# Layer A's probabilities, two heads of four turned by DMA as half-precision pairs

## The chip, the cores and the metric

The kernel runs on one core of one Trainium2 chip. The metric is the device time of one execution in microseconds; the time of a kernel is the median of its runs. A profile shows one execution, with the busy time of each engine: PE (TensorE, matmuls and the transposes made by matmul), PEld (its weight loads, which overlap), DVE (VectorE), ACT (ScalarE), POOL (GpSimd) and SP (SyncE, whose queue issues all of this kernel's DMAs).

## The reference

Two attention layers over 2048 prompt tokens and 64 sample tokens of width 1024. Each layer does `x + W_out(attn(RMSNorm(x)) * silu(gate))`, with q, k, v and gate from one input projection and RMS-normed q and k. Layer A (the one that changes) has 16 query heads on 2 key/value heads of width 64; a query of chunk c (64 tokens) sees its own chunk and the two before it, with a bucketed relative-position bias and a sink per head. Layer B has 16 heads with their own keys and values and sees 9 chunks.

```
def attend(q, k, v, bias, valid, sinks):
    s = jnp.einsum('bqkgd,bskd->bkgqs', qg, k).astype(jnp.float32) * (dh ** -0.5)
    s = s + bias.reshape(kv, g, tq, tk)
    s = jnp.where(valid, s, NEG_INF)
    sink = sinks.astype(jnp.float32).reshape(kv, g, 1, 1)
    m = jnp.maximum(jnp.max(s, axis=-1, keepdims=True), sink)
    p = jnp.exp(s - m)
    p = p / (jnp.sum(p, axis=-1, keepdims=True) + jnp.exp(sink - m))
    o = jnp.einsum('bkgqs,bskd->bqkgd', p.astype(v.dtype), v)
```

All arrays are float32. The kernel keeps that precision by holding a value as a high part (the value rounded to a matmul type) and a low part (what the rounding left), and by multiplying the parts.

## The kernel before

**Work items.** Layer A runs over four quarters of the heads (`qd`, four query heads each, two quarters to a key/value head) and, in each, over nine units: eight of 256 prompt tokens and one of the 64 sample tokens (`u == NU`). A prompt unit has two items of 128 tokens. That makes 64 prompt items and 4 sample items. All prompt items but the first tile of each quarter attend to two key tiles of 128 (their own and the one before); the four first tiles attend to one.

**The filler.** The projections run ahead of the attention and fill the gaps in it. `Filler` holds a generator of projection matmuls, and `filler.to(mark)` issues them on PE until the mark. PE's order is written out by hand (`manual_schedule` for PE); the instructions of the other engines and of the SP queue are put in order by the scheduler, from the order of the program and its simulated times, and then run in that order on their engine.

**One iteration of layer A's `pipeline`**, for item i: `scores(items[i])`; projections up to 0.3 of the iteration; `values(items[i-1])`; projections; in the first quarter `keys(items[i+2])`; projections up to 0.8; `turned(items[i+2], items[i-1])`; projections up to 0.95; `outputs(items[i-1])`; projections to the end.

- `scores`: 8 matmuls into two PSUM banks (tag `sa`), then for heads 0 and 1 and again for heads 2 and 3 the minimum with the bias and the sink on DVE (line 1213), and the exponential on ACT (line 1219), which writes p in float32 and adds up each row. Each pair of heads has one `p` tile; there are three `p` buffers.
- `values`: for each key tile 4 transposes on PE (line 904, 128x128 in float32) into one `sa` bank, then the high part by ACT (`ph`, line 871) and the low part by DVE (`pl`, line 872), for all four heads at once.
- `outputs`: for each key tile two matmuls of 512 columns (lines 1255 and 1256), with the values as the stationary operand. The values are held in one tile with high and low halves, both float32r (`VT`), so that rows 0 to 63 of the result hold the high half's product and rows 64 to 127 the low half's. `finish_pairs` adds the two, multiplies by the gate (line 1316 on POOL) and stores the result.
- `turned`: transposes of q and of the gate, their evacuation, and two small DMAs of q (line 1171) for item i+2.

The first projection, `first`, runs at the start, and `take_kv` splits the values by ACT and POOL (`split_v`, lines 847 and 848).

**Layer B** already holds its probabilities, in seven of its eight head pairs, in the other form: ACT writes the high part in float16 (line 1554), POOL the low part (line 1555), and one DMA with transposition (line 1563, tile `pt`) turns both; line 1660 multiplies them with values in float16. There the products come three steps after the DMA is asked for.

Of the kernel before, what the change touches and what calls it, by code (L numbers as in the profile page):

```python
# [9 lines left out]
F32 = mybir.dt.float32  # L10
# [43 lines left out]
TURNED = (0, 1)  # L54

@with_exitstack
def hybrid_encoder_kernel(
# [104 lines left out]
    row = const([P, 64], "scrow")[0:1]  # L162
    scanned, pending = [], []
# [697 lines left out]

    KA = const([P, SEQ], "KA", F16)
    KB = const([P, SEQ], "KB", F16)
    VT = t("values", [P, NT, 2, P], 1, F32R)
# [14 lines left out]

    def split_at(x, c):  # L880
        return x[:, :c], x[:, c:]
# [43 lines left out]
    held["chain"] = []  # L925
# [48 lines left out]
    def layer_a():  # L974
# [4 lines left out]
        def add_unit(qd, place, unit):  # L979
# [30 lines left out]
            def take_kv(it, ps):  # L1010
# [4 lines left out]
                split_v(n, v, VS[:, 1] if last else VT[:, tt])  # L1015
# [23 lines left out]
            def first():  # L1039
# [85 lines left out]
        def turned(it, done):  # L1125
# [13 lines left out]
            if done is not None:  # L1139
                done.gt = gate_t(tp[:, 256 : 256 + 2 * m].rearrange("p (j s) -> p j s", j=2), m)  # L1140
# [32 lines left out]
        def scores(it):  # L1173
# [33 lines left out]
            for j in range(2):  # L1207
# [4 lines left out]
                for h in (2 * j, 2 * j + 1):  # L1212
# [4 lines left out]
                    )  # L1217
                for h in (2 * j, 2 * j + 1):
# [4 lines left out]
            bg.anchor(mi, ex)  # L1223
            nc.vector.reciprocal(sm[:n], sm[:n])
# [7 lines left out]

        def values(it):
            qd = it.qd
# [13 lines left out]
        def outputs(it):  # L1248
# [5 lines left out]
            for c, (vt, kn) in enumerate(it.vts):  # L1254
                nc.tensor.matmul(O[:, : 4 * n], vt, hi[c], start=c == 0, stop=False)
                nc.tensor.matmul(O[:, : 4 * n], vt, lo[c], start=False, stop=c == m - 1)  # L1256
# [9 lines left out]
        def pipeline():  # L1266
            N = len(items)
            for i in range(-3, N + 1):
# [10 lines left out]
                filler.to(c0 + 0.3 * (end - c0))  # L1279
                if 0 <= i - 1:  # L1280
# [747 lines left out]
```

## Time and profile before

| | |
|---|---|
| Time, median of 3 runs | 2119.95 us (2118.64 to 2123.06) |
| The profiled execution | 2123.14 us, span 2121.3 us |
| Layer A's first quarter, with the start | 0 to 200 us of the span |
| Layer A's other three quarters | 200 to 645 us |
| Layer A's output projection | 645 to 870 us |
| Layer B's attention | 870 to 1970 us, then its output projection |
| Busy over the span | PE 96%, DVE 71%, ACT 68%, POOL 54% |
| Mean granted TensorE clock | 0.991 |

In a group of instructions the columns are line, engine, operation, output and inputs, shapes and count, then the busy time in microseconds and the mean of one in nanoseconds, then the idle time before them. In a timeline they are the start and the length in microseconds. A matmul's bar is longer than the time for which it holds the array, since matmuls are pipelined; the distance between starts tells what one costs.

### The profile page before, as it was taken

To read this page: it belongs to the slowest core of one execution; us is meant where nothing else is said; L and a number is where in the kernel's file an instruction comes from. 1 tells how busy PE (TensorE), PEld (TensorE's weight loads), DVE (VectorE), ACT (ScalarE), POOL (GpSimd) and SP (SyncE) were. 2 spreads that over 40 slices of the span, in tenths; PEclk is the share of its full clock that TensorE was granted. 3 is DMA by queue.
4 is the path that set the end of the run, shared out by engine and by line. 5 is a ranking of instruction groups with operands and counts; after the bars stand their busy time and mean duration, and the time that the engine had idled before them with its cause. 6 is when DMAs were issued, how large, how long until landed. Compare 5 with 4: busy or idle time off the path is not lost.

```text
span 2121.3 us, 40864 instructions
## 1 busy us (share of the span) xinstructions
PE 2046.8 (96%) x12951; PEld 1470.7 (69%) x12951; DVE 1498.7 (71%) x4049; ACT 1440.8 (68%) x3640; POOL 1143.7 (54%) x1621
## 2 busy tenths in 40 slices
PE   8999999999999999998999999999999999999999
PEld 6788788878888999655655555555555555557788
DVE  7778778768667554687768777787877778678542
ACT  6878878767777332466677677786867777677330
POOL 5655544433445445775367576676766767575000
PEclk9999999999999999999999999999999999999999
DMA  8856545766544666744469789897897969678763
GB/s 276 274 172 213 173 157 189 215 174 212 165 149 132 212 205 200 247 148 155 138 166 225 175 191 232 169 239 180 199 216 169 254 159 212 152 152 197 215 200 115
DMA packets 509593, 404.21 MB, mean 191 GB/s; under 512 B 302064, under 2 KB 446848, under 8 KB 509344
## 3 DMA queue, kind: packets, MB, share of 16 engines
q1 hardware_dynamic: 509376, 401.60, 70.1%
q8 instruction: 102, 1.67, 0.3%
q14 instruction: 115, 0.94, 0.1%
HBM read 257.59 MB, written 73.43 MB: 156 GB/s over the span
## 4 chain that ended last, share of the span: by engine, by line
PE 59%; DVE 12%; ACT 10%; DMA 6%; issue 6%; POOL 5%; SPq 0%; ACTq 0%; POOLq 0%; DVEq 0%
PE pj L713 10%; PE pj L715 10%; PE pj L714 10%; PE pj L1871 5%; PE pj L1873 5%; PE pj L1872 5%; PE o L1660 2%; PE sa L904 2%; PE tp L904 2%; DVE p L1502 2%; ACT values L1554 2%; PE sb L1498 2%; ACT p L1514 1%; PE sb L1499 1%; PE o L1256 1%
## 5 line engine op out<-in xcount | busy, mean ns | idle before, releaser
L713 PE MATMUL pj<-wh,xx 128*128 128x512 f16 (+2 forms) x1648 | 641.9, 389 | 6.0 <-ACT pb L736 2.3
L715 PE MATMUL pj<-wh,xx 128*128 128x512 f16 (+2 forms) x1648 | 624.3, 379 | 1.3 <-POOL xx L598 1.3
L714 PE MATMUL pj<-wh,xx 128*128 128x512 f16 x1024 | 389.4, 380 | 0.8 <-DVE wh L503 0.8
L1555 POOL TENSOR_TENSOR values<-p,values 128x640 f16<-128x640 f32 (+2 forms) x224 | 281.5, 1259 | 177.5 <-ACT values L1554 172.9
L1514 ACT ACTIVATE p<-p,nm 128x640 f32<-128x640 f32 (+5 forms) x264 | 199.3, 755 | 199.5 <-DVE nm L1507 150.3
L1871 PE MATMUL pj<-xx,wh 128*128 128x264 f32 (+1 forms) x1024 | 291.4, 285 | 8.4 <-DVE res L1877 3.9
L1872 PE MATMUL pj<-xx,wh 128*128 128x264 f32 (+1 forms) x1024 | 288.9, 282 | 0.0
L1502 DVE CUSTOM_DVE_ANT_0 p<-sb,BT 128x640 f32<-128x640 f32 (+5 forms) x272 | 196.6, 723 | 94.8 <-PE sb L1499 91.1
L714 PE MATMUL pj<-wl,xx 128*128 128x512 f32 (+1 forms) x624 | 234.6, 376 | 3.0 <-DVE wl L503 3.0
L598 POOL TENSOR_TENSOR xx<-xraw,xx 128x528 fp32r<-128x528 f32 (+4 forms) x144 | 185.4, 1305 | 90.8 <-ACT xx L597 84.1
L813 POOL TENSOR_TENSOR f<-f,mhalf 128x4 f32<-128x4 f32 (+2 forms) x187 | 190.4, 1019 | 11.8
L715 PEld LDWEIGHTS <-xx 128*128 128x128 f16 x1024 | 100.5, 98 | 124.5 <-issue 2.8
L1316 POOL TENSOR_TENSOR o<-gt,o 128x256 f32<-128x256 f32 (+1 forms) x132 | 103.6, 784 | 152.2 <-ACT p L1219 92.5
L818 DVE TENSOR_TENSOR pa<-pa,f 128x256 f32<-128x256 f32 (+3 forms) x221 | 145.6, 661 | 54.4 <-POOL f L813 49.9
L795 POOL TENSOR_TENSOR sq<-pa 128x256 f32<-128x256 f32 (+2 forms) x187 | 115.0, 615 | 115.1 <-ACT pa L749 80.1
L1219 ACT ACTIVATE p<-p,nm 128x257 f32<-128x257 f32 (+2 forms) x272 | 134.4, 497 | 47.4 <-DVE nm L1213 40.0
L714 PEld LDWEIGHTS <-xx 128*128 128x128 f16 x1024 | 100.5, 98 | 82.5 <-issue 4.7
L713 PEld LDWEIGHTS <-xx 128*128 128x128 f16 x1024 | 100.6, 98 | 80.7 <-ACT xx L597 1.5
L1554 ACT CAST values<-p 128x640 f16<-128x640 f32 (+2 forms) x224 | 147.3, 658 | 5.0
L1873 PE MATMUL pj<-xx,wl 128*128 128x264 f32 x512 | 145.8, 285 | 0.5 <-DVE wl L496 0.5
L1873 PE MATMUL pj<-xx,wh 128*128 128x264 f16 x512 | 142.7, 279 | 1.0 <-DVE wh L493 1.0
L1213 DVE CUSTOM_DVE_ANT_0 p<-sa,BT,nsink 128x256 f32<-128x256 f32 (+2 forms) x272 | 117.5, 468 | 35.7 <-PE sa L904 29.8
(282 smaller groups left out, 5028.9 us busy)
## 6 DMA issues: line engine op xcount, KB each, us to landing
xx<-xsb SPq DMA_DIRECT2D x112, 512.0 KB, 4.3
xx<-xsa SPq DMA_DIRECT2D x88, 512.0 KB, 4.7
xraw<-oga SPq DMA_DIRECT2D x64, 264.0 KB, 3.8
xraw<-ogb SPq DMA_DIRECT2D x64, 264.0 KB, 3.9
xsa<-xx SPq DMA_DIRECT2D x32, 512.0 KB, 4.3
wl<-in_w_in_b_dram SPq DMA_DIRECT2D x64, 256.0 KB, 5.0
wraw<-in_w_in_b_dram SPq DMA_DIRECT2D x56, 256.0 KB, 3.6
xraw<-in_x_dram SPq DMA_DIRECT2D x40, 256.0 KB, 4.2
```

Of the source, the lines that this page charges most:

```text
L598: nc.gpsimd.tensor_tensor(lo, rv, wide(hi), op=ALU.subtract)
L713: nc.tensor.matmul(ps[:n, :C], xh, wh, start=k == 0, stop=False)
L714: nc.tensor.matmul(ps[:n, :C], xh, wl, start=False, stop=False)
L715: nc.tensor.matmul(ps[:n, :C], xl, wh, start=False, stop=k == KC - 1)
L813: nc.gpsimd.tensor_tensor(fv, fv, mhalf[:n, :H], op=ALU.pow)
L1502: mi = nc.vector.tensor_tensor_reduce(out=p[r, :nk], in0=S[r, o : o + nk], in1=b, op0=ALU.add, op1=ALU.min, scale=1.0, scalar=3e38, accum_ ...
L1514: ex = nc.scalar.activation(p[:n, :nk], p[:n, :nk], AF.Exp, scale=-1.0, bias=it.nm[:n, c : c + 1], accum_out=it.sm[:n, c : c + 1],)
L1554: hi = nc.scalar.copy(two[:, :, 0, :], pv)
L1555: lo = nc.gpsimd.tensor_tensor(two[:, :, 1, :], pv, two[:, :, 0, :], op=ALU.subtract)
L1871: nc.tensor.matmul(ps[:, :OT], wh, oh, start=k == 0, stop=False)
L1872: nc.tensor.matmul(ps[:, :OT], wh, ol, start=False, stop=False)
L1873: nc.tensor.matmul(ps[:, :OT], wl, oh, start=False, stop=k == KC - 1)
```

## The change

For prompt items the probabilities of heads 0 and 1 (`TURNED_A = (0,)`, the first pair) no longer go through PE. After the exponential ACT copies them to float16 into a ring of three places, POOL writes the low part beside them, and one DMA with transposition on SP (`turn_a`) turns both parts of both heads: 4 m blocks of 128x128 for m key tiles. It is issued in the item's own iteration, ahead of `values` of the item before. Heads 2 and 3 are still transposed on PE, into one bank for both key tiles, and split by ACT and DVE, now into float16. `outputs_a` has matmuls of 256 columns in float16: first those of heads 2 and 3, high and low part and key tile by key tile, then those of heads 0 and 1 that read the turned tile.

The exponent gets log(2^14) added on DVE (one small instruction for each pair of heads), so that p is scaled; the row sums take up the same factor. The values are held as float16 high and low parts with one scale for the tensor, a power of two from the largest entries of the value weights (`value_top`, `value_across`, `value_scales`, all in the first unit and at the start of the second); the gate takes it out again. Since that scale is not known in the first unit, the value splits of its two tiles are put off to the second. They are now made by ACT and DVE. The tile `values` has the same bytes as before; its second half is the ring. Sample items are as before.

```diff
+    def value_top(ws):
+        for c, (w, _) in enumerate(ws[::2]):
+            nc.vector.tensor_reduce(
+                most[:, 80 + c : 81 + c], w.h[:, :, P:].bitcast(F32), axis=AX.XY, op=ALU.max,
+                apply_absolute_value=True,
+            )
+        nc.vector.tensor_reduce(
+            top[:, 10:11], most[:, 80:84], axis=AX.X, op=ALU.max, apply_absolute_value=True
+        )
+
+    def value_across():
+        ps = tp_bank()
+        nc.tensor.transpose(ps[0:1, 0:P], top[:, 10:11], ident)
+        m, e, r, o = row[:, 40:41], row[:, 41:42], row[:, 42:43], row[:, 44:46]
+        nc.vector.tensor_reduce(m, ps[0:1, 0:P], axis=AX.X, op=ALU.max)
+        nc.vector.tensor_scalar(m, m, 1e-12, 1.0, op0=ALU.max, op1=ALU.mult)
+        powers(m, e, r)
+        times(o[:, 0:1], r, VB)
+        times(o[:, 1:2], e, 0.5 / VB)
+
+    def value_scales():
+        ps = tp_bank()
+        nc.tensor.matmul(
+            ps[:, 0:2], ones[0:1, 0:1].to_broadcast([1, P]), row[:, 44:46], start=True, stop=True
+        )
+        nc.vector.tensor_copy(sva, ps[:, 0:2])
...
-    VT = t("values", [P, NT, 2, P], 1, F32R)
+    V16, ring = split_at(t("values", [P, 4 * NT * P], 1, F16), 2 * NT * P)
+    VT = V16.rearrange("p (a b c) -> p a b c", b=2, c=P)
+    held["ring"] = 0
...
-                split_v(n, v, VS[:, 1] if last else VT[:, tt])
+                if last:
+                    split_v(n, v, VS[:, 1])
+                else:
+                    held["v"].append((VT[:, tt], v.rearrange("p (h d) -> p h d", d=HD)))
+                if u == 1 and it is mine[0]:
+                    value_scales()
+                while u and held["v"]:
+                    vt, vv = held["v"].pop(0)
+                    split_to(vt[:, :, 0:HD], vt[:, :, HD:P], vv, sva[:, 0:1])
...
+                    if i == 5:
+                        value_top(st.wkv)
                     if i == 7:
                         token_scales(unit, xc, tp_bank())
...
                 for it, o in zip(mine, qgs):
                     take_qg(it, o[0])
+                value_across()
...
+                if u != NU:
+                    mi = nc.vector.tensor_scalar(
+                        nm[:, 2 * j : 2 * j + 2], nm[:, 2 * j : 2 * j + 2], math.log(PB), 1.0,
+                        op0=ALU.add, op1=ALU.mult,
+                    )
...
+            if u != NU:
+                held["ring"] = r = (held["ring"] + 1) % 3
+                m = nk // P
+                it.two = two = ring[:, 1024 * r :][:, : 512 * m].rearrange(
+                    "p (c l h k) -> p l c h k", c=m, l=2, h=2
+                )
+                for y, j in enumerate(TURNED_A):
+                    hi, lo = (two[:, l, :, 2 * y : 2 * y + 2] for l in range(2))
+                    pv = it.pe[j][:, :, :nk].rearrange("p h (c k) -> p c h k", k=P)
+                    nc.scalar.copy(hi, pv)
+                    nc.gpsimd.tensor_tensor(lo, pv, hi, op=ALU.subtract)
+                it.two = ring[:, 1024 * r :][:, : 512 * m]
...
+        def turn_a(it):
+            if it.unit[0] == NU:
+                return
+            it.pt = t("pt", [P, 2 * HALF], 2, F16)[:, : it.two.shape[1]]
+            nc.sync.dma_start_transpose(it.pt.rearrange("p (c q) -> p c q", q=P), it.two)
+
+        def values_a(it):
+            m = len(it.vts)
+            ph, pl = (t(x, [P, 5, 256], 2, F16) for x in ("ph", "pl"))
+            it.hi, it.lo = [], []
+            heads = [h for h in range(4) if h // 2 not in TURNED_A]
+            if heads:
+                PT = psum_a("sa", 512, 4)
+                PTv = PT.rearrange("p (c h k) -> p c h k", c=2, h=2)
+                for c in range(m):
+                    for x, h in enumerate(heads):
+                        transpose(PTv[:, c, x], it.pe[h // 2][:, h % 2, c * P : (c + 1) * P])
+                a, b = (x.rearrange("p a b -> p (a b)")[:, : m * 256] for x in (ph, pl))
+                bg.anchor(*split_to(a, b, PT[:, : m * 256]))
+                it.hi, it.lo = ([x[:, 256 * c : 256 * c + 256] for c in range(m)] for x in (a, b))
+
+        def outputs_a(it, O):
+            m = len(it.vts)
+            w = 256
+            heads = [h for h in range(4) if h // 2 not in TURNED_A]
+            todo = []
+            for c, (vt, kn) in enumerate(it.vts):
+                for l in range(2):
+                    if heads:
+                        todo.append((O[:, heads[0] * P : heads[0] * P + 256], vt, (it.hi, it.lo)[l][c]))
+                    todo.append(
+                        (O[:, 2 * P * TURNED_A[0] :][:, :w], vt, it.pt[:, (2 * c + l) * w : (2 * c + l + 1) * w])
+                    )
+            todo.sort(key=lambda x: x[2].tensor is it.pt.tensor)
+            for y, x in enumerate(todo):
+                nc.tensor.matmul(*x, start=y == 0, stop=y == len(todo) - 1)
...
                 filler.to(c0 + 0.3 * (end - c0))
+                if 0 <= i < N:
+                    turn_a(items[i])
                 if 0 <= i - 1:
                     values(items[i - 1])
```

More of the change, by code (lines that the diff above doesn't have):

```diff
@@ L54 @@
 TURNED = (0, 1)
+TURNED_A = (0,)
 @with_exitstack
@@ L162, in hybrid_encoder_kernel @@
     row = const([P, 64], "scrow")[0:1]
+    sva = const([P, 2], "sva")
     scanned, pending = [], []
@@ L922, in low_queries @@
         return Q2[turn[0] % 2]
-    held["chain"] = []
+    held["chain"], held["v"] = [], []
     class Filler:
@@ L1139, in turned @@
             if done is not None:
-                done.gt = gate_t(tp[:, 256 : 256 + 2 * m].rearrange("p (j s) -> p j s", j=2), m)
+                done.gt = gate_t(
+                    tp[:, 256 : 256 + 2 * m].rearrange("p (j s) -> p j s", j=2), m,
+                    0.5 if done.unit[0] == NU else sva[:, 1:2],
+                )
             if it is not None:
@@ L1253, in outputs @@
             m = len(it.vts)
-            for c, (vt, kn) in enumerate(it.vts):
-                nc.tensor.matmul(O[:, : 4 * n], vt, hi[c], start=c == 0, stop=False)
-                nc.tensor.matmul(O[:, : 4 * n], vt, lo[c], start=False, stop=c == m - 1)
+            if it.unit[0] != NU:
+                outputs_a(it, O)
+            else:
+                for c, (vt, kn) in enumerate(it.vts):
+                    nc.tensor.matmul(O[:, : 4 * n], vt, hi[c], start=c == 0, stop=False)
+                    nc.tensor.matmul(O[:, : 4 * n], vt, lo[c], start=False, stop=c == m - 1)
             finish_pairs(
```

7 lines of the change are left out of this document (5 added, 2 removed).

## The prediction

> **What bounds the kernel now.** I read the page's engine totals first, then layer A's two stretches, then PE's starts in time.
>
> ```profile
> PE 2046.8 (96%) x12951; PEld 1470.7 (69%) x12951; DVE 1498.7 (71%) x4049; ACT 1440.8 (68%) x3640; POOL 1143.7 (54%) x1621
> core 0: us, PE busy (x) PEld busy (x) DVE busy (x) ACT busy (x) POOL busy (x), PEclk, DMA share, GB/s
> 0.00:200.00 200.00, 185.45 (x1101) 155.91 (x1102) 147.36 (x522) 157.34 (x423) 113.76 (x172) 0.98 0.73 232
> 200.00:645.00 445.00, 439.98 (x2412) 356.26 (x2411) 325.59 (x958) 341.03 (x952) 200.00 (x383) 0.99 0.59 179
> ```
>
> From 200 to 645 us, layer A's last three quarters, PE has 5 us idle in 445, while ACT is busy 77% (341.03/445), DVE 73%, POOL 45% and DMA 59%. Busy bars overlap, so the starts have to say whether the array itself is full. One item, from its scores to the next item's scores:
>
> ```profile
> 401.68 0.39 PE L1255 MATMUL o<-ph,values 128*128 128x512 f32 x1
> 401.91 0.39 PE L1256 MATMUL o<-pl,values 128*128 128x512 f32 x1
> 402.14 0.28 PE L1202 MATMUL sa<-KB,q 128*128 128x256 f16 x1
> 402.26 0.27 PE L1203 MATMUL sa<-KB,q 128*128 128x256 f16 x1
> 402.37 0.27 PE L1202 MATMUL sa<-KB,q 128*128 128x256 f16 x1
> ...
> 405.10 1.03 PE L904 MATMUL sa<-ident,p 128*128 128x128 f32 x8
> 405.89 0.48 PE L713 MATMUL pj<-wh,xx 128*128 128x512 f32 x1
> 406.20 0.39 PE L714 MATMUL pj<-wl,xx 128*128 128x512 f32 x1
> ...
> 409.87 0.39 PE L1255 MATMUL o<-ph,values 128*128 128x512 f32 x1
> ...
> 410.81 0.28 PE L1202 MATMUL sa<-KB,q 128*128 128x256 f16 x1
> ```
>
> A float32r matmul of 512 columns costs 0.23 us (401.68 to 401.91), a float16 one of 256 columns 0.11 (402.26 to 402.37). Eight transposes with the projection matmul behind them take 1.10 (405.10 to 406.20), so 0.87 without its 0.23: 0.109 each. The item lasts 8.67 (402.14 to 410.81), and its work adds up to that: 24 projections at 0.23 (5.52), 8 scores (0.88), 8 transposes (0.87), 4 of q and gate (0.44), 4 products (0.92): 8.63. PE is full; its time is the stage's time.
>
> **What the change takes from PE.** A full prompt item loses 4 of 8 transposes, 4 x 0.109 = 0.44. Its 4 products at 0.23 (0.92) become 8 at 0.11 (0.88): 0.04 less. Together 0.47. There are 15 full items in each quarter, 60 x 0.47 = 28.2; the four with one key tile give half, 1.0. The sum is **29 us** off PE.
>
> The Trainium skill (TensorE: Matmul & The Clock Gate, Part 4: PE-mode transpose) gives about 275 ns for one such transpose inside a kernel; by that price the 248 removed would be 68 us. The row of this trace has that length as the bar's, and the starts decide:
>
> ```profile
> L904 PE MATMUL sa<-ident,p 128*128 128x128 f32 x496 | 64.5, 272 | 0.0
> ```
>
> **What it moves to the other engines.** Layer B does the same steps, so most have a row.
>
> ```profile
> L871 ACT CAST ph<-sa 128x512 fp32r<-128x512 f32 x124 | 68.0, 588 | 19.7 <-PE sa L904 19.0
> L872 DVE TENSOR_TENSOR pl<-sa,ph 128x512 fp32r<-128x512 f32 x124 | 81.0, 681 | 0.7 <-ACT ph L871 0.4
> L1554 ACT CAST values<-p 128x640 f16<-128x640 f32 x168 | 121.7, 724 | 3.7
> L1555 POOL TENSOR_TENSOR values<-p,values 128x640 f16<-128x640 f32 x168 | 237.2, 1415 | 127.5 <-ACT values L1554 123.4 <-issue 1.3 <-DMA pt<-values 1.1
> L1507 DVE TENSOR_SCALAR nm<-nm 128x1 f32<-128x1 f32 x224 | 32.0, 143 | 1.1
> ```
>
> Per full item ACT swaps one of two high parts (588 ns) for the copy of p: 512 columns, some 0.58 by 724 x 512/640. Nothing. DVE loses one low part (681) and gains two additions (2 x 143): 0.39 less. POOL gains 1415 x 512/640 = 1.13. Over an item of 8.67 - 0.47 = 8.20, POOL goes from 3.90 (45% of 8.67) to 5.03, 61%; ACT stays at 6.68, 81%; DVE falls to 72%. All are covered by PE's 8.20. The value splits shift about 0.3 us each, 16 times, from POOL to DVE, once in the kernel.
>
> DMA needs a sum. Two stretches of 300 us, layer A's first (300 to 600) and layer B's second (1100 to 1400), and the start (30 to 130):
>
> ```profile
> q1 hardware_dynamic: 38468, 55.49, 61.2%
> q1 hardware_dynamic: 109331, 58.71, 86.4%
> pt<-values SPq DMA_TRANSPOSE x74, 4.0
> q1 hardware_dynamic: 19122, 26.64, 82.2%
> ```
>
> Layer A's plain traffic takes 183.6 us (61.2%) for 55.49 MB, 3.3 us per MB. In layer B 74 turns of at most 0.33 MB (128 x 640 x 2 parts x 2 bytes) are some 24 MB; the other 34.5 cost 114 us, which leaves 145 of 259 for the turns, about 2.0 each. Layer A's is 0.26 MB: 1.55 us of all engines, per item 18% more. After 200 us DMA goes from 59% to about 80%, under the 86% with which layer B runs. In the start it goes from 82% to 96% (an item there has 24 projections of 512 columns and 24 of 256, some 11 us: 14%). That is the one place where I charge for it: 100 us hold 9 items, 14 us of transfers into 18 us of slack. I take **3 us**, from 0 (all fits) to 10 (most of it stalls PE).
>
> The Trainium skill (DMA: Bandwidth & Descriptors, Latency and other measured facts) gives 261 GB/s for a transposing DMA on non-contiguous data; by that the turn would take 1.0 us and the start would reach only 91%, and I would charge nothing there. The trace's 0.33 MB in 2.0 us is dearer, and I keep it.
>
> **When the turned tile lands.** `outputs` now waits on a DMA, in PE's order, and everything on PE stands behind it. ACT and POOL at the same item, layer B's turn, and its landing:
>
> ```profile
> 407.60 0.20 ACT L1219 ACTIVATION_READ_ACCUMULATOR p<-p,nm 128x1 f32 x1
> 408.22 0.61 POOL L1226 TENSOR_TENSOR G<-pb,sm 128x256 f32<-128x256 f32 x1 [1.65 <-DVE sm L1224]
> 408.79 0.61 POOL L795 TENSOR_TENSOR sq<-pa 128x256 f32<-128x256 f32 x1
> 410.37 1.01 POOL L813 TENSOR_TENSOR f<-f,mhalf 128x4 f32<-128x4 f32 x1
> L1563 SPq DMA_TRANSPOSE pt<-values x224: 1167/1363/5339, 1059.6 to 1964.1; - x112
> DMA to landing us min/median/max: 2.3/3.7/9.2
> ```
>
> The exponentials of the item scored at 402.14 end at 407.8. The copy ends at 408.4 (0.58), the low part at 409.5 (1.13), or near 411 if POOL has G and the square first. SP then spends 1.36 on the issue, and landing takes 3.7 in the median: 413 to 416. The item's products stand one item after 409.87, at 418.5. So the chain is 11 to 14 us long and may be 16.4, which is 1.89 periods; at the new 8.20 it may be 15.5. Usually covered by 2 to 4 us; the 9.2 us landing overshoots. Behind the turn on SP wait the loads of `xx`, q and bias rows and the stores of `oga`, by about 1.4 us of issue and what POOL is late; they are asked for a unit or an item ahead. POOL's G, squares and powers wait 1.1 longer behind the low part; what they feed, `turned`, comes most of an item later. For such small lateness I take **2 us**, from 0 to 8. Below nothing is possible too: a turned `p` tile comes free without waiting for line 904 in the next item, and the second pair's softmax can start earlier; since PE is full that earns no time.
>
> **The start.** Four reductions of 256 columns, a small one, a transpose, six tiny DVE steps, a matmul and a copy come in before the second unit's values. The nearest rows:
>
> ```profile
> L809 DVE TENSOR_REDUCE f<-sq 128x4 f32<-128x256 f32 x176 | 72.3, 414 | 24.1 <-POOL sq L795 23.8
> 12.28 0.15 DVE L143 TENSOR_SCALAR qsc<-qkg 128x2 f32<-128x2 f32 x1
> 28.75 0.50 PE L714 MATMUL pj<-wl,xx 128*128 128x512 f32 x1 [2.97 <-DVE wl L503]
> ```
>
> 4 x 0.41 + 8 x 0.15 = 2.8 us of DVE, where PE already waits 2.97 for DVE. I take **3 us**; 0 if the reductions fall into DVE's gaps, 6 if PE's transpose and matmul wait for the tiny steps as well.
>
> **The sum.** 29 - 3 - 2 - 3 = 21 us less. The profiled execution, 2123.14 with a span of 2121.3, lies 3.2 above the median of 2119.95; 2123.14 - 21 = 2102 on its own footing, and on the median's, which I predict, **2099 us**. With every charge at nothing it is 2091; with all at their ends (10, 8, 6) 2115.
>
> **The rivals.**
>
> ```profile
> SPq L1563 <- POOL G L1539: 71.0, 24, 5.0
> who waited for it (us, times):
>   ACT o L1311: 12.1, 10
>   POOL values L1555: 1.1, 1
> ```
>
> *The turn decides (slower).* Place: the wait for `pt` ahead of `outputs_a`'s last four matmuls. Each period is then the chain divided by 1.89. From 15.5 us of mean chain on PE waits, and from 16.4 on (8.67 an item) the change loses. With landings near 7 us instead of 3.7, an SP queue that holds the turn back 1 us, and POOL's late case, 14 becomes 18.3; then the period would be 9.68, and 62 items x (9.68 - 8.67) = +63, with the start's 3 some 2186. A milder case, chain 17 and period 9.0, gives 62 x 0.33 + 3 = +23: 2143, the price I put on it. For it: SP's order is fixed ahead, and in layer B SP stands waiting for POOL in front of line 1563. Against it: among those that wait for layer B's `pt`, the last rows above, there is no PE, at a higher DMA load, though with three steps between. 15%.
>
> *PE is not the bound (no change).* ACT, DVE and their handoffs set the item, and what PE saves turns into waits: 29 - 29, with the start's 3 and the DMA's -2 at most, 2120 to 2125; I put 2121. PEld is busy only 356 of 445 us, 80%. Against it: starts 0.23 apart in a row and 8.63 of 8.67 accounted for. The Trainium skill (Trainium Kernel Development and Optimization, Best Practices) has the rule behind it: judge by weight loads, not by matmul busy time. By that, a fifth of the stage would be open. The starts don't bear it out. 7%.
>
> *The half-precision products cost more (smaller gain).* Eight matmuls load weights eight times. If each cost 0.17 instead of 0.11, the 0.47 would vanish; line 1202's starts, each with its own weights, speak against it. 3%, near 2121 too.
>
> **Chances.** Forecast 75%, of which all is faster. Turn decides 15%, slower. No gain 10%: half within 0.2% (4 us, about what a measurement of this kernel can tell from no change), a third slower, the rest faster. So faster 0.77, same 0.05, slower 0.18. The range runs from 2089 (all charges nothing, less 2 for the spread of runs) to 2125, which takes in the no-gain cases and leaves out the turn's.
>
> **What the changed profile would show.** Line 904's `sa` transposes by 248 fewer; the item from scores to scores near 8.2 us; line 1660's kind of row, 256 columns, 0.11 apart; no PE wait on `pt` above 2 us in all; POOL near 60% and DMA near 80% after 200 us; PE's starts lagging by about 3 us after the first 40. Wrong would be a PE idle row released by `pt` or by `xx`, or an item still at 8.6.

## The result, and the profile after

The changed kernel takes 2129.19 us (median of 5 runs, 2128.62 to 2134.18), the kernel before 2118.64 (5 runs beside them, 2115.68 to 2123.06). The ratio is 1.0055, 95% interval 1.0037 to 1.0073: slower, where 2099 us was forecast, with a range of 2089 to 2125. The profiled execution of after is one of 2129.19 us, with a span of 2127.4 and a granted clock of 0.992.

The page's engine totals of after:

```profile
PE 2021.7 (95%) x12954; PEld 1442.1 (68%) x12954; DVE 1506.4 (71%) x4145; ACT 1440.7 (68%) x3644; POOL 1215.0 (57%) x1669
```

The two stretches of layer A, with the columns shown before (us, then busy time and instructions of PE, PEld, DVE, ACT and POOL, then granted clock, DMA share, GB/s):

```profile
0.00:200.00 200.00, 176.31 (x1085) 146.88 (x1086) 153.72 (x561) 157.57 (x421) 124.97 (x169) 0.99 0.85 247
200.00:645.00 445.00, 421.17 (x2411) 334.73 (x2410) 322.61 (x1002) 336.65 (x947) 250.35 (x426) 1.00 0.76 205
```

PE is busy for 25 us less in the whole span (29 were worked out). But from 200 to 645 us, with nearly the same number of matmuls (2411 and 2412), it is busy for 421 us where it was for 440, in the same 445. The saving turned into waits. What PE waited for in that stretch (us in total, times, longest):

```profile
PE o L1330 <- DMA pt<-values: 7.5, 6, 1.6
PE tp L935 <- DVE pa L847: 6.5, 6, 3.3
PE o L1330 <- DVE pl L906: 5.3, 13, 0.7
```

In the names, `pa` is the q of a coming item, which DVE multiplies by its norm before PE transposes it for `turned`, and `pb` is its gate. None of these three rows stood in that table of before but `pa`, once, with 2.4 us. One item of the last quarter, scores to scores, shows the commonest of them (timeline of after: start, length):

```profile
592.75 0.27 PE L1247 MATMUL sa<-KB,q 128*128 128x256 f16 x1
...
596.24 0.48 DVE L1258 CUSTOM_DVE_ANT_0 p<-sa,BT,nsink 128x256 f32<-128x256 f32 x1
...
596.65 0.69 DVE L1264 TENSOR_SCALAR nm<-nm 128x2 f32<-128x2 f32 x2
...
597.37 0.51 ACT L1269 ACTIVATE p<-p,nm 128x257 f32<-128x257 f32 x1 [0.86 <-DVE nm L1264]
...
598.86 0.50 ACT L1269 ACTIVATE p<-p,nm 128x257 f32<-128x257 f32 x1
...
599.36 0.56 ACT L905 CAST ph<-sa 128x512 f16<-128x512 f32 x1
...
599.95 0.69 DVE L906 TENSOR_TENSOR pl<-sa,ph 128x512 f16<-128x512 f32 x1
...
600.70 0.27 PE L1330 MATMUL o<-pl,values 128*128 128x256 f16 x1 [0.31 <-DVE pl L906]
...
601.46 0.27 PE L1247 MATMUL sa<-KB,q 128*128 128x256 f16 x1
```

Both additions stand on DVE behind all four minima (596.65). The exps of the first pair wait for them and then run four in a row to 599.3. The cast of the other pair's high part comes behind the exps, the low part behind the cast, and the products of the item before wait for the low part. Then come the next scores, 8.71 after the last ones. There is no wait on the turned tile in this quarter. In before, each of the first pair's exps started right behind its own minimum, and the casts of the high parts came between the two pairs (the item of the prediction, scored at 402.14):

```profile
404.01 0.08 DVE L1213 DVE_READ_ACCUMULATOR2_ANT nm<- 128x1 f32 x1
...
404.19 0.51 ACT L1219 ACTIVATE p<-p,nm 128x257 f32<-128x257 f32 x1 [0.86 <-DVE nm L1213]
...
405.73 1.07 ACT L871 CAST ph<-sa 128x512 fp32r<-128x512 f32 x2 [0.45 <-PE sa L904]
...
405.95 0.48 DVE L1213 CUSTOM_DVE_ANT_0 p<-sa,BT,nsink 128x256 f32<-128x256 f32 x1 [0.23 <-PE sa L904]
...
406.69 0.52 ACT L1219 ACTIVATE p<-p,nm 128x257 f32<-128x257 f32 x1
```

By line and shape, the additions, the exps of the full items, the transposes left on PE and the new work on ACT and POOL:

```profile
L1264 DVE TENSOR_SCALAR nm<-nm 128x2 f32<-128x2 f32 x128 | 39.1, 327 | 0.6
...
L1269 ACT ACTIVATE p<-p,nm 128x257 f32<-128x257 f32 x240 | 119.9, 502 | 59.2 <-DVE nm L1264 57.1 <-POOL p L1256 1.7 <-POOL f L842 0.4
...
L935 PE MATMUL sa<-ident,p 128*128 128x128 f32 x248 | 37.4, 272 | 0.0
L1283 ACT CAST values<-p 128x512 f16<-128x512 f32 x60 | 36.7, 612 | 0.1
...
L1284 POOL TENSOR_TENSOR values<-p,values 128x512 f16<-128x512 f32 x60 | 70.7, 1179 | 5.6 <-ACT values L1283 4.2 <-DMA row<-vec 0.7
```

An addition took 327 ns in the mean, not the 143 that it was priced at, and ACT stood 57.1 us in front of the exps until an addition was done (in before 38.2 us, until a minimum was). The casts and the low parts lie near the forecast 580 and 1130 ns, and the transposes are the 248 fewer. The queue's shares of DMA time, from 300 to 600 us and from 30 to 130:

```profile
q1 hardware_dynamic: 71018, 64.83, 79.7%
q1 hardware_dynamic: 24317, 27.43, 92.6%
```

### The profile page after: what moved, and what is told of

Same layout as the page of the kernel before. It is cut to its first block, busy times and chain, and to the rows that moved or that the text cites. A ratio compares the mean times of both kernels' runs of the same rounds, so it can differ in the third digit from the quotient of the medians.

```text
span 2127.4 us, 41090 instructions
## 1 busy us (share of the span) xinstructions
PE 2021.7 (95%) x12954; PEld 1442.1 (68%) x12954; DVE 1506.4 (71%) x4145; ACT 1440.7 (68%) x3644; POOL 1215.0 (57%) x1669
## 4 chain that ended last, share of the span: by engine, by line
PE 46%; DVE 17%; ACT 12%; DMA 9%; issue 8%; POOL 6%; SPq 1%; ACTq 0%; POOLq 0%; DVEq 0%
PE pj L742 7%; PE pj L744 7%; PE pj L743 7%; PE pj L1977 4%; PE pj L1979 4%; PE pj L1978 4%; PE o L1766 3%; ACT p L1269 2%; DVE p L1258 2%; PE sb L1604 2%; PE sb L1605 2%; DVE pa L847 2%; DVE p L1608 2%; DVE o L1421 1%; PE tp L935 1%
## 5 line engine op out<-in xcount | busy, mean ns | idle before, releaser
L847 DVE TENSOR_TENSOR pa<-pa,f 128x256 f32<-128x256 f32 (+3 forms) x221 | 150.0, 680 | 56.6 <-POOL f L842 50.3
L824 POOL TENSOR_TENSOR sq<-pa 128x256 f32<-128x256 f32 (+2 forms) x187 | 116.6, 624 | 98.9 <-ACT pa L778 79.7
L742 PEld LDWEIGHTS pj<-wh,xx 128*128 128x128 f32 x624 | 117.7, 189 | 25.0 <-ACT pb L765 7.5
```

The lines of the kernel that those rows point to most:

```text
L742: nc.tensor.matmul(ps[:n, :C], xh, wh, start=k == 0, stop=False)
L847: nc.vector.tensor_tensor(sv, sv, fv.unsqueeze(2).to_broadcast([n, H, HD]), op=ALU.mult)
```

## The experiments

Two theories stood at the beginning. **Theory A**: the loop scores, minima, additions, exps, cast, low part, products, next scores became longer than PE's work, because the exps wait for the additions. **Theory B**: the turn by DMA is what is late, by its own length and by SP's order. Ratios are to the kernel before on the same chip.

**Without the two additions** (noadd):

```diff
-                if u != NU:
-                    mi = nc.vector.tensor_scalar(
-                        nm[:, 2 * j : 2 * j + 2], nm[:, 2 * j : 2 * j + 2], math.log(PB), 1.0,
-                        op0=ALU.add, op1=ALU.mult,
```

> Leaves out the two additions of log(2^14) per prompt item, so layer A's p is not scaled. Theory A (a loop of handoffs sets the item: scores, minima and additions on DVE, all four exponentials on ACT, then the cast ph, then pl on DVE, then the products and the next scores): the first pair's exponentials start 2 us earlier, and items of the last quarter fall from 8.70 to 8.2-8.4 us; about 15 us less than the changed kernel, near 2113. Theory B (the turn: SP's queue, the DMA load and the wait for pt set it): no change, near 2129.

2118.73 us, 0.9981 (0.9971 to 0.9991), and the last quarter's items last 8.2 us instead of 8.7. Two instructions of a third of a microsecond are worth 0.74%, some 16 us. In the profiled executions of after and noadd these lie in the second quarter (8.7), the last (2.8) and the stretch between layer A's last item and layer B's first turn (5.3); so the loop of the steady items is shown for a part of them.

**The second pair's softmax asked for after `values`** (split):

```diff
-            for j in range(2):
+            def pair(j):
...
+            pair(0)
...
+            def second():
+                pair(1)
...
                     values(items[i - 1])
+                if 0 <= i < N:
+                    second()
```

> The second pair's softmax is asked for after the split of the item before (values), and the turned pair's copy and low part follow the first pair's exponentials at once; the order on PE is the same. Theory A: the cast ph stands between the two pairs' exponentials on ACT, as before the change; the wait for pl goes, items of the last quarter at 8.2-8.3 us, near 2110. Theory B: only the turn is earlier; the waits for pt in the third quarter (some 9 us) go, the last quarter stays at 8.70, near 2123.

A miss: 2133.85 us, 1.0051 (1.0036 to 1.0067), items still 8.7. In its trace DVE's order still has both additions together behind the fourth minimum. ACT's order did follow: the cast of the high part now stands between the two pairs of exps. But the first pair's exps still wait for the additions, and so the cast starts 6.6 us after the item's scores, as in after, and the products still wait for the low part. The order in the program fixed the order on one engine and not on the other, and the run left the wait as it was.

**Layer B's bias rows moved out of the third quarter** (spread), into layer A's output projection:

```diff
-                        if qd == 2 and 1 <= place <= 4:
-                            spread(1, place - 1)
...
+                    if layer == 0 and half == 0 and m == 1 and j < 7:
+                        spread(1, j, 2)
```

> Layer B's bias rows are spread (32 DMAs of 191.5 KB) during layer A's output projection instead of its third quarter, so that SP and the DMA engines are freer beside the turns. Theory A: the pt waits of the third quarter go, but its items then meet the same loop at 8.7: 5 us less, near 2124. Theory B: 10 us or more less, 2119 or below.

2137.11 us, 1.0068 (1.0055 to 1.0082). The third quarter's mean item (its length over its 17 items, the sample item among them) went from 8.93 to 8.63 us, so the rows do stand in its way, but the output projection lost more than that.

**Without the turn by DMA** (noturn; the products read the parts unturned):

```diff
-            it.pt = t("pt", [P, 2 * HALF], 2, F16)[:, : it.two.shape[1]]
-            nc.sync.dma_start_transpose(it.pt.rearrange("p (c q) -> p c q", q=P), it.two)
+            it.pt = it.two
```

> Leaves out the DMA with transposition: the products read the unturned parts from the ring, so these two heads' products are of other data; everything else is there. Theory A: no wait for pt, but items of the last quarter still take 8.70: near 2124. Theory B: what the change takes from PE comes through: near 2100.

2131.15 us, 1.0032 (1.0019 to 1.0045); the last quarter stays at 8.7. The turn explains a small part only, as theory A has it.

**The first pair's addition ordered ahead of the second pair's minima** (addorder):

```diff
+                    if u != NU and h == 2:
+                        behind(mi.ins, add.ins)
```

> All computation of the changed kernel is kept; on VectorE the second pair's two minima are ordered behind the first pair's addition, which stands behind both minima of its pair, so that the first pair's exps can start while the second pair's minima are still being made. Theory A (the loop scores, four minima, both additions, four exps, cast, low parts, products, next scores sets the item): the exps of the first pair start about 1 us earlier (two minima of 0.4 us and an addition of 0.33), the cast of the second pair's high parts with them, the last quarter's period falls from 8.70 to about 8.2 to 8.3, the waits of the exps on nm from 57 to under 25 us, and the time to about 2113 to 2117. Rival (it is the additions' own time on VectorE, 39 us in all, not their place): the period stays near 8.7 and the time near 2129.

The last quarter's steady items fell to 8.2 to 8.3 us, as theory A said, and yet the time was 2132.88, 1.0062 (1.004 to 1.0085). In its trace the earlier quarters are longer: PE waits 7.4 us for `pa` and 7.2 for the turned tile from 200 to 645 us, and the first quarter's items last 11.69 us in the mean where they last 11.23 in after. What follows is narrower than hoped: the loop in the steady items is mended, and the earlier quarters lose more than the last one gains. The edit makes DVE's order stiffer everywhere; whether that is the reason isn't shown.

**The kernel before with the two additions alone** (before_add):

```diff
+                if u != NU:
+                    mi = nc.vector.tensor_scalar(
+                        nm[:, 2 * j : 2 * j + 2], nm[:, 2 * j : 2 * j + 2], math.log(PB), 1.0,
+                        op0=ALU.add, op1=ALU.mult,
```

> The kernel before with nothing changed but the two additions to nm, one per pair, ahead of the exps; the probabilities are then larger by a constant factor that the division by their sum takes out. Theory A: there the loop has a slack of its own (the exps of the first pair start right behind two minima, and PE is full), so that the additions take a part of it and the rest is lost: the period of the last quarter rises by 0 to 0.6 us, the time to between 2119 and 2140, and if the additions stand behind all four minima here too, to about 2135. Rival (the additions cost only together with the cast and the low parts of the second pair): no change, 2119.

2131.84 us, 1.0067 (1.0046 to 1.0087). The additions cost some 14 us in the old kernel as well. Here, though, the steady items stayed at 8.7. In the profiled execution, 6 us longer than that of before, the loss lies in the first quarter (11.87 us an item for 11.38), with PE waiting for `pl`, `pb` and `pa`.

**A constant value scale** (const), with no work for it at the start:

```diff
+    nc.vector.memset(sva[:, 0:1], 64.0)
+    nc.vector.memset(sva[:, 1:2], 0.5 / 64.0)
...
-                    value_scales()
...
-                        value_top(st.wkv)
...
-                value_across()
```

> The changed kernel with the value scale a constant, 64, and its two reciprocal factors constants too: no largest value is taken, none is handed across the partitions, and the values are split as they arrive. What the start's added work costs: theory A and the prediction's working expect 3 to 5 us less than the changed kernel, about 2125, with PE's waits in the first 200 us down by as much (on pb, on the projection weights' maxima, on scrow). Rival (the start is bound by its transfers, 92.6% of the DMA time between 30 and 130 us, and the scale costs nothing): 2129.

2130.81 us, 1.0052 (1.0037 to 1.0068): no gain. The start's added work costs nothing that can be measured.

**Without the additions, and bias rows two heads to an item** (noadd_lazy), each skewed store asked for an item after its load:

```diff
-            st = store(skew[layer, h], row)
...
+            held["rows"].append((skew[layer, h], row))
...
-                        if qd == 0 and 1 <= place <= 3:
-                            spread(0, place)
+                        if qd == 0 and 1 <= place <= 7:
+                            spread(0, 2 * place + 2, 2 * (place < 7))
...
-                        if qd == 2 and 1 <= place <= 4:
-                            spread(1, place - 1)
+                        if qd == 2 and place >= 1:
+                            spread(1, 2 * place - 2)
```

> The changed kernel without the two additions, and with the bias rows asked for two heads to an item instead of four, each skewed store asked for one item after its load, so that SyncE does not stand before the turn in line until a row has landed. Theory A (the third quarter's waits on the turned tiles, 7.5 us of PE in the changed kernel, come from SyncE's order and not from the turn's own length): the third quarter's mean period falls from 8.9 to 8.3 to 8.5 and the time lies 3 to 6 us under the same kernel with the rows as they were (0.998 of before), at about 2109 to 2112. Rival (the rows' transfers themselves, or what moves with them, are what is late): same as without the rows spread, about 2114.

2109.53 us, 0.9956 (0.9941 to 0.997), about 5 us under the run without the additions alone. The edit thins out layer A's rows in the first quarter as well as layer B's in the third. The third quarter's mean item is 8.63 instead of 8.90 (8.3 to 8.5 were expected), and no wait on the turned tile is left in PE's table from 200 to 645 us. What the rows do is plain in the trace of after (SP and POOL, one item of the third quarter):

```profile
406.63 1.15 POOL L1284 TENSOR_TENSOR values<-p,values 128x512 f16<-128x512 f32 x1
...
409.14 2.65 SPq L360 DMA_DIRECT2D row<-vec  x2
...
411.84 1.29 SPq L1216 DMA_DIRECT2D q<-q  x2
...
413.18 1.33 SPq L1299 DMA_TRANSPOSE pt<-values  x1
...
417.73 0.60 PE L1330 MATMUL o<-pt,values 128*128 128x256 f16 x4 [1.25 <-DMA pt<-values]
```

Both parts are there at 407.8. SP has rows and q in front and issues the turn at 413.2, and PE waits for it.

**The rows alone, in the kernel before** (before_lazy), the same edit:

> The kernel before with the bias rows asked for two heads to an item and each skewed store one item after its load, as in the run without the additions. Theory A (SyncE's order matters through the turn alone, which this kernel doesn't have): no change, 0.999 to 1.001. Rival (the rows' order helps any kernel of this kind): about 0.997, 2114.

2119.43 us, 0.9988 (0.9974 to 1.0001): not to be told from no change.

**The additions kept, into a tile that nothing reads** (dummy):

```diff
-                        nm[:, 2 * j : 2 * j + 2], nm[:, 2 * j : 2 * j + 2], math.log(PB), 1.0,
+                        unread[:, 2 * j : 2 * j + 2], nm[:, 2 * j : 2 * j + 2], math.log(PB), 1.0,
```

> The changed kernel with the two additions still made on VectorE, at their place and from the same minima, but into a tile that nothing reads, so that the exps start from the plain minima. It parts two readings of what the additions cost. Latency (the exps, and with them the cast, the low parts and the products, start later): the cost is gone, about 0.998 of before as without the additions, 2117, last quarter's period about 8.2. VectorE's own time (39 us of it, with everything that stands behind in its order: low parts, norms, splits of weights): the cost stays, about 1.0055, 2130, with PE's waits on pa and pl as in the changed kernel.

2119.61 us, 0.9988 (0.9975 to 1.0002), steady items 8.2 us. DVE made all 128 additions, in the last quarter behind all four minima as in after, and 434 ns each in the mean, and the cost was gone. It is the exps' wait that costs.

**The additions on GpSimd** (pooladd):

```diff
-                    mi = nc.vector.tensor_scalar(
+                    nc.gpsimd.tensor_scalar(
```

> The changed kernel with the two additions made by GpSimd instead of VectorE; the exps still wait for them, through one more engine. Latency reading: the exps start as late or later (the pair's minima, a handover, the addition on GpSimd of some 0.2 to 0.3 us, a handover, and whatever GpSimd has in hand), so the time is 2129 or more, up to 2145, period of the last quarter 8.7 or more. VectorE's own time: VectorE is freed of 39 us and the time comes back to about 2117 to 2120.

2122.04 us, 0.9992 (0.9977 to 1.0007): the cost is gone here too, against what the latency reading expected. The timeline of its last quarter says why:

```profile
599.66 0.08 DVE L1258 DVE_READ_ACCUMULATOR2_ANT nm<- 128x1 f32 x1
...
599.84 0.19 POOL L1264 TENSOR_SCALAR nm<-nm 128x2 f32<-128x2 f32 x1 [2.47 <-DVE nm L1258]
...
600.06 0.52 ACT L1269 ACTIVATE p<-p,nm 128x257 f32<-128x257 f32 x1 [1.38 <-POOL nm L1264]
...
601.53 0.19 POOL L1264 TENSOR_SCALAR nm<-nm 128x2 f32<-128x2 f32 x1
```

On GpSimd each pair's addition stands right behind its own minima, and the exps start 0.40 us after the second minimum (599.66 to 600.06), not behind two more minima, two additions of `o` and both additions of `nm`. Latency is the mechanism, as dummy shows. What made it long was mostly the place in DVE's order: in the item of after above, the second minimum of the first pair was read at 594.96, and the first exp started at 597.37. Of these 2.4 us the two additions took 0.69, part of it held up by POOL (last section). The run's expectation had taken the extra handover for the larger part. ACT's idle time in front of the exps is no measure of the cost: with the additions on GpSimd it is 71.4 us in all, more than the 57.1 of after.

**The kernel before with 28 us less on PE** (lesspe):

```diff
-                nc.tensor.matmul(O[:, : 4 * n], vt, hi[c], start=c == 0, stop=False)
+                whole = it.unit[0] == NU
+                if whole:
+                    nc.tensor.matmul(O[:, : 4 * n], vt, hi[c], start=c == 0, stop=False)
```

> The kernel before without the products of the high parts in layer A's items of 128 query rows: 2 x 0.233 us of TensorE less for each of 60 items, the change's own saving, and nothing else changed (the products of the low parts wait for the same tiles). What a saving on TensorE of 28 us is worth by itself. The prediction's step (TensorE sets the pace of layer A, every us off it counts): 2092 to 2095, ratio 0.987. Rival of the prediction (TensorE isn't the bound; the other engines' order sets the item): 2112 to 2121, ratio 0.996 to 1, with new waits on pl, pa and pb for what it saves.

2096.82 us, 0.9879 (0.986 to 0.9899): 25.7 of the 28 us come back. In the kernel before, PE is what bounds layer A.

The missing part now has a size, 0.9879 against 0.9956, but no owner; the next kernels look for it.

**Neither additions, nor parts, nor turn** (notwo_lazy), in noadd_lazy:

```diff
-                    nc.scalar.copy(hi, pv)
-                    nc.gpsimd.tensor_tensor(lo, pv, hi, op=ALU.subtract)
...
-            nc.sync.dma_start_transpose(it.pt.rearrange("p (c q) -> p c q", q=P), it.two)
+            it.pt = it.two
```

> The changed kernel without the additions and with the thinner rows, and beyond that without the casts and subtractions that make the two half-precision parts and without the turn by DMA; the products of the turned pair read a constant area of zeros. What is left is the saving on TensorE and the value scale at the start. If the missing 16 us go to the two parts and the turn: 0.988 to 0.990, 2092 to 2098. If they go to the value scale and the later start of the values, or are not there to be had with the shorter PE work of this layout: 0.994 to 0.996, 2107 to 2112.

2092.31 us, 0.9872 (0.9857 to 0.9888). The layout's saving on PE is all there to be had.

**The parts made, not turned** (noturn_lazy), with the edit of noturn in noadd_lazy:

> As the kernel without the additions and with the thinner rows, but without the turn by DMA alone: the two parts are still made, and the products of the turned pair read them unturned (wrong data, the same work on TensorE). If the two parts' work on ScalarE and GpSimd takes the missing time (36.7 and 70.7 us in the changed kernel, through later casts of the other pair and later gate products): 0.994 to 0.996, no change to speak of against the kernel with the turn. If the turn and its traffic take it (waits on pt, on q and on xx): 0.988 to 0.991.

2106.61 us, 0.9931 (0.9918 to 0.9944). It lies between the two readings: making the parts costs 0.59%, the turn 0.25%. The steady items are 8.2 us long in both kernels, and the items that differ much are two: 12.4 for 8.2 us in the second quarter, 13.2 for 9.2 in the last. The first of them is one in which POOL also makes low parts of the input (`xx`, line 630, four of 1.3 us), here without (first) and with the parts (second):

```profile
265.10 1.26 POOL L845 TENSOR_TENSOR f<-f,mhalf 128x4 f32<-128x4 f32 x1
...
266.39 0.42 DVE L850 TENSOR_TENSOR pa<-pa,f 128x256 f32<-128x256 f32 x1 [0.57 <-POOL f L845]
...
267.31 0.38 PE L939 MATMUL tp<-ident,pa 128*128 128x128 f32 x2
```

```profile
265.50 0.61 POOL L1288 TENSOR_TENSOR G<-pb,sm 128x256 f32<-128x256 f32 x1
266.07 1.15 POOL L1284 TENSOR_TENSOR values<-p,values 128x512 f16<-128x512 f32 x1
267.18 1.01 POOL L845 TENSOR_TENSOR f<-f,mhalf 128x4 f32<-128x4 f32 x1
...
268.22 0.42 DVE L850 TENSOR_TENSOR pa<-pa,f 128x256 f32<-128x256 f32 x1 [2.29 <-POOL f L845]
...
268.80 0.41 PE L938 MATMUL tp<-ident,pa 128*128 128x128 f32 x2 [2.96 <-DVE pa L850]
```

The power of the norm stands behind G and the low part on POOL, `pa` behind the power, and PE waits 2.96 us for `pa`. In the other item PE waits 3.62 us for the low part `pl`, which DVE makes behind two splits of weights (2.93 us); by what path the parts put it there isn't shown.

**All computation kept, additions on GpSimd, thinner rows** (pooladd_lazy): the edits of pooladd and noadd_lazy (its rows, not its additions).

> The changed kernel with all its computation, the two additions made by GpSimd and the bias rows asked for two heads to an item with each skewed store one item after its load. Both mended places together: additions on GpSimd gave 0.9992, thinner rows gave 0.0025 without the additions. Theory A expects 0.996 to 0.997, about 2113, third quarter's waits on the turned tiles (6.4 us with the rows as they were) nearly gone and its mean period 8.6. Rival (a turn that SyncE asks for in time is still late, since the exps start 0.4 us later by way of GpSimd): 0.999.

2113.62 us, 0.9967 (0.9955 to 0.9979): faster than both kernels, with the scaling kept. PE's waits on the turned tile fell from the 6.4 us of pooladd to 1.7, and the third quarter's mean item from 9.18 to 8.76.

**addorder with thinner rows** (addorder_lazy):

> The changed kernel with all its computation, the first pair's addition ordered on VectorE ahead of the second pair's minima, and the thinner rows. If the loss of the run without thinner rows (1.0062 in spite of a last-quarter period of 8.25) sits in the rows' traffic in front of the turn: 0.998 to 1.000, third quarter's mean period from 9.2 to 8.6. If it sits in VectorE's fixed order itself (minima held behind an addition, norms and low parts behind them): 1.003 to 1.006.

2132.07 us, 1.0048 (1.0033 to 1.0063), third quarter's mean item still 9.24. The rows are not what addorder loses by. That DVE's fixed order does it in some other way is argued from the waits on `pa`; it isn't shown.

**The account.** Each row takes one thing more away; 0.1% is 2.1 us, and each step is uncertain by some 4 us, from the two intervals, so that the two steps of 5.3 are hardly above it.

| kernel | ratio | the step is worth |
|---|---|---|
| the change's saving on PE alone (notwo_lazy) | 0.9872 | -27 us |
| and the two parts made (noturn_lazy) | 0.9931 | +12.5 |
| and the turn (noadd_lazy) | 0.9956 | +5.3 |
| and the rows four heads to an item (noadd) | 0.9981 | +5.3 |
| and the two additions on DVE (after) | 1.0055 | +15.7 |

The steps depend on the order in which they are taken; in after, taking the turn away gave 4.9 us (1.0055 to 1.0032).

## Why the prediction was wrong

**PE is full, and 29 us come off it: right.** lesspe gives 25.7 us for 28, notwo_lazy 27. The item is 8.2 us long wherever nothing else is late, the very 8.20 of the prediction, so the starts (0.109 for a transpose, 0.11 for a product) priced the work well.

**The step that failed is "All are covered by PE's 8.20".** It set busy time in an item against the item's length: ACT 81%, DVE 72%, POOL 61%. From 200 to 645 us after they are 76%, 72% and 56%, no higher than forecast. But an engine at 72% can still hold up a full one if what PE waits for next stands late in its order. The row for two additions had them at 2 x 143 ns and, set against the low part saved, as a gain of 0.39 us of DVE; they measured 327 each, and cost 15.7 us. Even the size is not the point: dummy makes the same additions, longer ones at that, at no cost. The prediction never asked where they stand on DVE and who waits behind them, which was the question to ask of an added instruction between the minima and the exps. Both of the text's signs of being wrong came: items of 8.7 us, and a row of PE waiting for `pt`, 7.5 us.

**The slack that was there went too.** The text had it that the second pair's softmax can start earlier, "since PE is full that earns no time". It can also use up slack. In before, ACT cast the high parts between the two pairs of exps, 3.6 us after the item's scores (405.73); the second pair waited for a `p` tile until PE's transposes were done. With the tile free early, ACT runs all four exps first and casts behind them. In noadd the cast starts 5.2 us after the scores, and the items last 8.2: so far it takes no time. With the additions it starts 6.6 us after them (599.36 above), and PE waits.

**POOL's low part: "covered", measured 12.5 us with the casts.** The text said that what G, squares and powers feed comes most of an item later. That holds in steady items and fails in one in which POOL also makes low parts of the input (4.2 us). In the other long item (4.0 us) PE waits for `pl` behind splits of weights on DVE; what makes it so, and the rest of the 12.5, stays open.

**The turn: mechanism right, 2 us charged, 5 measured, and 5 more from SP's order.** The turn's own rows in after, issue (ns) and landing:

```profile
L1299 SPq DMA_TRANSPOSE pt<-values x64: 1190/1274/2468, 56.5 to 691.4; - x64
...
DMA to landing us min/median/max: 2.4/3.6/6.8
```

Issue 1.27 and landing 3.6 are near the 1.36 and 3.7 of layer B (the landing is counted from the start of the issue, so the forecast's 416 has the issue in it twice). From scores to landing it is mostly 11.5 to 15 us, for 11 to 14 forecast, and 15 to 21 in many items of the first and third quarters. The rival of the deciding turn (chain 17, 2143) did not come about: the time went its way, slower, but the last quarter's items are 8.7 us long without any wait on the turned tile. The bias rows were named among what waits behind the turn. That the turn also waits behind them was not.

**DMA shares: right** (79.7% for about 80, 92.6% for 96). **The start's 3 us for the scale: not found** (const). The start's 3 us for transfers were not measured by themselves; PE's waits in the first 200 us are not on a DMA but for 1.2:

```profile
PE pj L742 <- ACT pb L765: 5.9, 5, 2.9
PE tp L935 <- DVE pa L847: 5.3, 4, 2.8
...
PE sa L1247 <- DMA q<-q: 1.2, 1, 1.2
```

**The rivals.** The nearest was that PE isn't the bound, at 7% and 2121. Of the kernel before it is untrue (lesspe). The change made it true, by lengthening the loop, and it then cost more than the saving, which the rival didn't allow for: it gave back 29 at most.

## What to carry to other kernels

A full engine's saving counts only if nothing it waits for moves later by more than its slack; so for each added instruction follow its place in its engine's order to the next wait of the full engine, and don't set busy shares against the period. A small operation between two long ones on different engines can be better put on the engine whose order has it right behind its inputs: here, moving two additions from DVE to GpSimd was worth as much as leaving them out, within the interval. And an edit to the order of the program is to be looked up in the trace, since the order on the engine may not have followed.

## What the runs showed of the hardware

*A small operation on DVE can be held until POOL is done.* The same addition took 0.17 us in one place and 0.43 in another of addorder's items (DVE and POOL):

```profile
597.73 0.17 DVE L1266 TENSOR_SCALAR nm<-nm 128x2 f32<-128x2 f32 x1
...
598.53 0.61 POOL L824 TENSOR_TENSOR sq<-pa 128x256 f32<-128x256 f32 x1
...
598.61 0.08 DVE L1258 DVE_READ_ACCUMULATOR2_ANT nm<- 128x1 f32 x1
598.73 0.43 DVE L1266 TENSOR_SCALAR nm<-nm 128x2 f32<-128x2 f32 x1
```

The long one started while POOL was at its square and ended with it (599.14 and 599.16). In dummy the two additions together lasted about as long as POOL's low part beside them:

```profile
600.08 1.17 POOL L1285 TENSOR_TENSOR values<-p,values 128x512 f16<-128x512 f32 x1
...
600.10 1.25 DVE L1265 TENSOR_SCALAR unread<-nm 128x2 f32<-128x2 f32 x2
```

In after, 86 of the 128 additions took at most 0.22 us, and 42 took 0.29 to 1.26; each of these 42 ended 0.02 to 0.03 us after an operation of POOL did. Against the 0.16 us of the short ones, that makes some 21 of the additions' 39.1 us. Of those right behind an accumulator's read the middle one took 0.17, so the read isn't what makes them long. On GpSimd an addition took 0.19.

*A wait of PE can be dearer than itself.* In before, one of PE's two long waits between 200 and 645 us:

```profile
217.95 0.66 PE L904 MATMUL tp<-ident,pa 128*128 128x128 f32 x2 [2.39 <-DVE pa L818]
...
219.26 0.63 PE L714 MATMUL pj<-wl,xx 128*128 128x512 f32 x1
219.69 0.63 PE L715 MATMUL pj<-wh,xx 128*128 128x512 f32 x1
```

The windows of before, over the matmuls behind that wait (the columns as above; the granted clock is the last but two):

```profile
218.00:221.40 3.40, 3.40 (x11) 2.82 (x11) 3.29 (x8) 3.26 (x10) 0.61 (x1) 0.51 0.32 96
```

After 2.39 us of waiting the granted clock was 0.51 for 3.4 us, and matmuls of 512 columns started 0.43 apart instead of 0.23. The Trainium skill (TensorE: Matmul & The Clock Gate, Part 1: The HAM clock gate) has the half clock come after an idle window of about 3.4 us; here 2.39 us of one wait were enough. In noturn_lazy the clock was 0.50 for 3.4 us as well, from 269.7 us, behind the wait of 2.96 shown above; 2.2 us of that lie in its item, and at half the clock they account for about 1.1 of the 4.2 us by which it is longer, as an estimate from these numbers.
